# A two-layer trunk on one core: taps ahead of the heads, an end by tiles, meta values in fewer matmuls, meta rows on ACT, squares in other slots

## The chip, the cores and the metric

One core of one Trainium2 chip runs the whole program. The metric is the device time of one execution in microseconds. The engines are PE (matmuls; PEld is its weight load), DVE, ACT, POOL and SP, which here issues transfers; each works through its own list of instructions in the order in which the list was built, and waits for others by semaphores.

## The reference

512 tokens of 1024 features, with 16 learned meta tokens ahead of them (528 positions), go through an input norm and two layers. A layer is half a feed-forward net, a token mixer, and half a feed-forward net, each added to its scaled input and normed:

```
h = LN(alpha*h + 0.5*SwiGLU_1(h))
h = LN(alpha*h + W_out [pool | conv | retention](h))
h = LN(alpha*h + 0.5*SwiGLU_2(h))

z = h @ w_in                               # pool 256, conv 2 x 256, q, k, v, g 512 each
pool : trailing means over 2, 4, 8, 16 tokens minus the input, times w_pool
conv : u = a * sigmoid(gate); depthwise causal convolution, 31 taps; LN; silu; @ w_pw
ret  : 4 heads of 128; q, k turned by cos/sin; in chunks of 64 with decay;
       norm over the head; * gain * silu(g)
```

The meta tokens are dropped from the output. All is float32.

## The kernel before, in words

Activations lie with features on the partitions, and positions in two halves (s = 0 and 1) of 264 columns: 256 tokens and 8 meta columns. Every product of two float32 matrices is made of three matmuls: each operand is split into a high part, rounded to the matmul's format on ACT (L91, L315), and a low part, the difference, on DVE or POOL (L94, L320); then high x high, high x low and low x high are added in one PSUM bank (L133 to L135). PSUM has four banks under the tag "acc", two each under "att" and "stat". SBUF tiles come from pools by tag: 16 buffers of the tag "wide" (558 columns), 4 of "q", 5 of "sm", and so on. A tile that is asked for takes the buffer that comes free next, in the order in which the program asks.

The order on each engine is set when the program is built: a scheduler takes the instructions in the order of the code, with its own estimate of when each can start, and puts the ready ones into each engine's list. What the code yields and when (`PACE`) shifts them.

`enter` norms the input rows token by token; of two tiles of meta rows (8 rows each) it lets POOL do the scaling (L244), of the others DVE or ACT (L242, L246). PE turns them (L257). `center` norms features: sum over tiles, mean by a matmul (L283), centring on DVE (L289), squares on ACT into tiles of the tag "q" (L291), sums of the squares on POOL and DVE (L296, L298), variance by a matmul (L189).

The mixer makes first the pool and convolution inputs (m0pu, m0u), then the values v0 to v4, token tile by token tile: L680 to L682 multiply 128 tokens (v4: the 16 meta positions) with w_v, 8 x 3 matmuls of 512 columns. v4's tokens stand in small tiles xm, filled by POOL (L670). DVE sums each value tile over a head (L684), ACT centres it (L690). Then the heads run through `work`: per head two projections each for k and q (m0kp, m0qp: 24 matmuls of 264 columns), turned by `rotary` (ACT L701, L702, DVE L703 to L705), k's meta columns copied by POOL (L794, m0km), then scores (L719), decay on DVE (L730), values, gates (m0gp).

The convolution's 31 taps for two halves of 128 channels are 62 instructions on DVE (L608 the first two, L610 the others), each over 528 columns into m0y, a wide tile. `conv_taps` yields after each, and the loop over the heads takes `PACE[head]` of them per step of `work`: 4, 3, 3, 2 and 0. The pooling windows (L639, L642, on POOL; L645 to L647 on DVE) are sums of shifted copies. The layer 1 mixer (m1) does the same.

The last feed-forward net (`last_ffn`) turns h to token tiles first. Its five parts multiply hidden units with w2, both operands split; output columns are taken in two halves (`ch`), and in the last part the second half is done tile by tile (L888 to L890), DVE adding each product to yt (L894). Then `measure`, `root`, `scale` and `leave` norm each of the four token tiles and send it out (L938, L944, L948 to L956).

Of the kernel before, what the change touches and what calls it, by code (L numbers as in the profile page):

```python
# [58 lines left out]
def trunk(ctx, tc, a):  # L59
# [786 lines left out]
    def last_ffn(l, name):  # L846
# [18 lines left out]
        for part, units in enumerate(PARTS):  # L865
# [5 lines left out]
            nk = len(full)  # L871
            for ch in range(2):
# [24 lines left out]
                if part == len(PARTS) - 1 and ch == 1:  # L897

                    for tt in range(3):
                        for i in steps:  # L900
                            step(i, tt)
                        for j in range(2):
                            add(tt, j, ps[tt][:, j * 256 : (j + 1) * 256])
                    for j in range(2):
                        o = ps[3] if j == 0 else acc(f"{name}o{ch}4")
                        for i in steps:
                            step(i, 3, j * 256, 256, o[:, :256])
                        add(3, j, o[:, :256])
                else:
                    for i in steps:  # L910
                        for tt in range(4):
                            step(i, tt)
                    for tt in range(4):
                        for j in range(2):
                            add(tt, j, ps[tt][:, j * 256 : (j + 1) * 256])
# [158 lines left out]
```

## Time and profile before

| what | value |
|---|---|
| runs | 1963.27, 1964.85, 1964.92 us; median 1964.85 |
| the profiled execution | 1963.63 us; its span 1961.8 us |
| granted clock of PE, mean | 0.994 |
| PE busy | 1907.0 us, 97% of the span, 14471 matmuls |
| DVE busy | 1526.4 us, 78% |
| ACT busy | 909.2 us, 46% |
| POOL busy | 217.4 us, 11% |
| chain that ended last | PE 82%, DVE 11%, issue 2%, ACT 2%, POOL 2% |

The span is the profiled part of one execution; the time is some 1.8 us longer. The chain is the work that ended last, followed back step by step. Where an engine that is busy most of the span stands still, the row of the instruction behind the gap names what it waited for. An idle engine that nobody waits for costs nothing.

### The profile page before, as it was taken

What the parts mean: (1) busy time and instruction counts of PE and PEld (TensorE: products, weight loads), DVE (VectorE), ACT (ScalarE), POOL (GpSimd) and SP (SyncE); (2) the same over time, 40 slices, a digit from 0 to 9 for tenths busy, and PEclk for the clock granted to TensorE, in tenths of its full rate; (3) what the DMA queues carried; (4) which work ended last, traced back from release to release, by engine and by line L of the source; (5) the groups of instructions that cost most, each with busy time, mean ns of one, the idle gap of its engine ahead of it and who ended that gap; (6) DMA issues with size and microseconds to landing.
All of it is one profiled execution on the core that took longest, in us unless ns stands there. A gap on an engine that the chain in (4) does not pass through costs nothing.

```text
span 1961.8 us, 36780 instructions
## 1 busy us (share of the span) xinstructions
PE 1907.0 (97%) x14471; PEld 1824.0 (93%) x14471; DVE 1526.4 (78%) x3426; ACT 909.2 (46%) x1817; POOL 217.4 (11%) x283
## 2 busy tenths in 40 slices
PE   7999999999999999999999999999999999999996
PEld 6999999897899999999999999998889999999995
DVE  7788778689767887778696788787897686877787
ACT  5454446444333644455464454454343265544461
POOL 4000000442003000000120000005320130000001
PEclk9999999999999999999999999999999999999998
DMA  4422323322112223223223323332231213323321
GB/s 144 130 89 95 119 87 105 101 76 86 63 33 76 65 97 119 87 97 105 90 71 103 108 81 103 98 129 65 65 105 55 65 44 119 119 76 108 108 97 43
DMA packets 61068, 177.98 MB, mean 91 GB/s; under 512 B 6976, under 2 KB 10944, under 8 KB 60896
## 3 DMA queue, kind: packets, MB, share of 16 engines
q1 hardware_dynamic: 59744, 174.59, 27.9%
q8 instruction: 113, 1.85, 0.4%
q10 hardware_dynamic: 1152, 1.05, 0.2%
q14 instruction: 59, 0.48, 0.1%
HBM read 173.52 MB, written 2.10 MB: 90 GB/s over the span
## 4 chain that ended last, share of the span: by engine, by line
PE 82%; DVE 11%; issue 2%; ACT 2%; POOL 2%; DMA 0%; SPq 0%; DVEq 0%; POOLq 0%; ACTq 0%
PE f1bo L890 2%; PE f1bo L888 2%; PE f1bo L889 2%; PE f1a_y L134 2%; PE f0a_y L134 2%; PE f0b_y L134 2%; PE f1a_y L135 2%; PE f0b_y L133 2%; PE f0b_y L135 2%; PE f1a_y L133 2%; PE f0a_y L133 2%; PE f0a_y L135 2%; DVE m1y L610 1%; PE m1sc L719 1%; PE m0o L738 1%
## 5 line engine op out<-in xcount | busy, mean ns | idle before, releaser
L610 DVE SCALAR_TENSOR_TENSOR m1y<-m1u,vec,m1y 128x528 f32<-128x528 f32 x60 | 46.1, 803 | 0.0
L91 ACT CAST f0b_o_h<-f0b_o_r 128x512 fp32r<-128x512 f32 (+1 forms) x37 | 23.4, 636 | 48.7 <-PE f0b_y L134 29.6
L91 ACT CAST f0a_o_h<-f0a_o_r 128x512 fp32r<-128x512 f32 (+1 forms) x37 | 23.4, 635 | 48.6 <-PE f0a_y L134 29.5
L610 DVE SCALAR_TENSOR_TENSOR m0y<-m0u,vec,m0y 128x528 f32<-128x528 f32 x60 | 45.9, 801 | 0.0
L91 ACT CAST f1a_o_h<-f1a_o_r 128x512 fp32r<-128x512 f32 (+1 forms) x37 | 23.4, 636 | 48.4 <-PE f1a_y L134 29.6
L335 DVE TENSOR_TENSOR x<-x,f0a_y 128x264 f32<-128x264 f32 x64 | 27.2, 426 | 23.2 <-PE f0a_y L135 23.1
L335 DVE TENSOR_TENSOR h<-h,f1a_y 128x264 f32<-128x264 f32 x64 | 27.1, 425 | 23.1 <-PE f1a_y L135 23.0
L335 DVE TENSOR_TENSOR h<-h,f0b_y 128x264 f32<-128x264 f32 x64 | 27.1, 425 | 23.0 <-PE f0b_y L135 22.9
L94 DVE TENSOR_TENSOR f1bw_l<-f1bw_r,f1bw_h 128x512 fp32r<-128x512 f32 x42 | 27.7, 688 | 17.6 <-ACT f1bw_h L91 17.0
L949 POOL TENSOR_TENSOR yt<-yt,g_last 128x256 f32<-128x256 f32 x4 | 3.0, 739 | 333.2 <-ACT yt L948 333.2
L94 DVE TENSOR_TENSOR f0a_o_l<-f0a_o_r,f0a_o_h 128x512 fp32r<-128x512 f32 (+1 forms) x42 | 26.7, 642 | 13.8 <-ACT f0a_o_h L91 11.7
L94 DVE TENSOR_TENSOR f0b_o_l<-f0b_o_r,f0b_o_h 128x512 fp32r<-128x512 f32 (+1 forms) x42 | 26.6, 642 | 13.8 <-ACT f0b_o_h L91 11.7
L94 DVE TENSOR_TENSOR f1a_o_l<-f1a_o_r,f1a_o_h 128x512 fp32r<-128x512 f32 (+1 forms) x42 | 26.7, 642 | 13.7 <-ACT f1a_o_h L91 11.4
L278 POOL TENSOR_TENSOR f0b_ln_s<-h,h 128x264 f32<-128x264 f32 x2 | 1.6, 820 | 310.0 <-DVE h L335 310.0
L587 POOL MEMSET m0u<- 128x30 f32 x2 | 0.2, 123 | 304.0 <-PE f0a_20Q L135 304.0
L587 POOL MEMSET m1u<- 128x30 f32 x2 | 0.2, 123 | 303.1 <-PE f1a_20Q L135 303.1
L894 DVE TENSOR_TENSOR yt<-yt,f1bo 128x256 f32<-128x256 f32 x80 | 27.8, 415 | 5.4 <-PE f1bo L890 5.3
L91 ACT CAST f1bw_h<-f1bw_r 128x1024 fp32r<-128x1024 f32 (+1 forms) x22 | 22.1, 1011 | 21.1 <-PE f1bo L890 4.2
L291 ACT ACTIVATE m_ln_q<-h 128x264 f32<-128x264 f32 (+1 forms) x32 | 11.9, 414 | 39.7 <-DVE h L289 36.2
L257 PE MATMUL tr<-ident,xtok 128*128 128x128 f32 (+1 forms) x48 | 10.9, 328 | 11.9 <-DVE xtok L242 11.3
L257 PEld LDWEIGHTS tr<-ident,xtok 128*128 128x128 f32 (+1 forms) x48 | 6.8, 167 | 16.0 <-issue 14.7
L281 POOL TENSOR_TENSOR m_ln_s<-m_ln_s,h 128x264 f32<-128x264 f32 (+1 forms) x20 | 18.3, 914 | 30.8 <-DVE h L329 24.8
(10715 smaller groups left out, 9301.2 us busy)
## 6 DMA issues: line engine op xcount, KB each, us to landing
f1bw_r<-in_w2last SPq DMA_DIRECT2D x20, 512.0 KB, 3.9
f0a_o_r<-in_w SPq DMA_DIRECT2D x32, 256.0 KB, 2.7
f0b_o_r<-in_w SPq DMA_DIRECT2D x32, 256.0 KB, 2.8
f1a_o_r<-in_w SPq DMA_DIRECT2D x32, 256.0 KB, 2.8
m0wo_r<-in_w_out SPq DMA_DIRECT2D x8, 512.0 KB, 3.5
m1wo_r<-in_w_out SPq DMA_DIRECT2D x8, 512.0 KB, 3.5
m0w_r<-in_w_in SPq DMA_DIRECT2D x6, 512.0 KB, 4.0
m1w_r<-in_w_in SPq DMA_DIRECT2D x6, 512.0 KB, 4.2
```

The lines of the kernel that those rows point to most:

```text
L91: nc.scalar.copy(out=hi[:, :n], in_=w[:, :n])
L94: e.tensor_tensor(out=lo[:, sl], in0=w[:, sl], in1=raw(hi[:, sl]), op=ALU.subtract)
L133: nc.tensor.matmul(out, lhsT=wh, rhs=xh, start=start, stop=False, skip_group_check=onto)
L134: nc.tensor.matmul(out, lhsT=wh, rhs=xl, start=False, stop=False, skip_group_check=onto)
L135: nc.tensor.matmul(out, lhsT=wl, rhs=xh, start=False, stop=stop, skip_group_check=onto)
L335: nc.vector.tensor_tensor(out=y, in0=y, in1=ps, op=ALU.add)
L610: nc.vector.scalar_tensor_tensor(out=ys[c], in0=src, scalar=wk, in1=ys[c], op0=ALU.mult, op1=ALU.add)
L719: nc.tensor.matmul(sc[:kn, :cw], lhsT=kk[ks][:, kc : kc + kn], rhs=qq[s][:, c0 : c0 + cw], start=True, stop=True)
L888: nc.tensor.matmul(o, lhsT=hh, rhs=wh, start=part > 0 and i == 0, stop=False)
L889: nc.tensor.matmul(o, lhsT=hh, rhs=wl, start=False, stop=False)
L890: nc.tensor.matmul(o, lhsT=hl, rhs=wh, start=False, stop=i == nk - 1)
L894: nc.vector.tensor_tensor(out=y[:, :256], in0=y[:, :256], in1=o, op=ALU.add)
```

## The change

Five edits come together.

1. Taps: `EARLY` = 28 taps are made before the loop over the heads, and `PACE` becomes (1, 1, 2, 2, 0); inside the loop the taps are asked for behind the last rotary or gate (`issue_after`).
2. Meta values: xm holds high and low of the 16 meta positions side by side as 48 columns (16 high, 16 of zero, 16 low; the zeros are written by POOL, L666), so that v4 takes two matmuls per k instead of three; the low part's rows are then copied by ACT into a new wide tile m0vm and added by DVE.
3. Meta rows: in `enter` ACT scales them too, and the order within a group is turned round.
4. End by tiles: the last part's products run per token tile over both halves, followed at once by that tile's norm; tiles 0 to 2 leave by ACT, POOL (tile 2: DVE) and DVE, tile 3 by DVE, ACT and POOL.
5. Squares: every second square of a norm over more than two tiles takes a slot of the tag "sm", the one of the scores, instead of "q".

```diff
-PACE = (4, 3, 3, 2, 0)
+EARLY, PACE = 28, (1, 1, 2, 2, 0)
...
-            for i, tt in enumerate(group):
+            for i, tt in reversed(list(enumerate(group))):
...
-                elif i == 2:
-                    nc.gpsimd.tensor_scalar(out=y, in0=y, scalar1=mv[:p, i, 0:1], scalar2=rs[:p, i : i + 1], op0=ALU.subtract, op1=ALU.mult)
...
-            q.append(t(f"{name}_q{i}", "q"))
+            q.append(t(f"{name}_q{i}", "sm" if k > 2 and i % 2 else "q"))
...
-            pair = sq_pool.tile([P, 2, NM], F32R, tag="xm", name=f"{name}xm{k}", bufs=KT)
+            pair = sq_pool.tile([P, 48], F32R, tag="xm", name=f"{name}xm{k}", bufs=KT)
+            nc.gpsimd.memset(raw(pair[:, NM:32]), 0.0)
...
+                if tt == 4:
+
+                    nc.tensor.matmul(ps[:48], lhsT=xm[k], rhs=wh, start=k == 0, stop=False)
+                    nc.tensor.matmul(ps[:48], lhsT=xm[k], rhs=wl, start=False, stop=k == KT - 1)
+                    continue
...
+            if tt == 4:
+                vm = wide(f"{name}vm")
+                nc.scalar.copy(out=vm[:n, :512], in_=ps[32 : 32 + n])
+                nc.vector.tensor_tensor(out=vm[:n, :512], in0=ps[:n], in1=vm[:n, :512], op=ALU.add)
+                ps = vm[:, :512]
...
         taps = conv_taps()
+        for _ in range(EARLY):
+            next(taps)
...
-                for _ in range(PACE[hd]):
-                    next(taps, None)
                 if hd == HEADS or i > 0:
                     next(steps, None)
+                with tc.issue_after(made["last"]):
+                    for _ in range(PACE[hd]):
+                        next(taps, None)
...
+        c0 = done * 512
+        w_last = [[], []]
+        for i in range(0, nk, 2):
+            cw = min(2, nk - i) * 512
+            for ch, make in enumerate((weights, weights_wide)):
+                w = make(a["w2last"][ch, :, c0 + i * 512 : c0 + i * 512 + cw], cw, f"{name}l{ch}{i}")
...
         for tt in range(4):
+            ts = slice((tt % 2) * P, (tt % 2 + 1) * P)
+            for ch in range(2):
+                for c, cw in ((0, 256), (256, 256)) if (tt, ch) == (3, 1) else ((0, 512),):
+                    o = acc(f"{name}l{tt}{ch}{c}")
...
             measure(tt)
             root(tt)
-            if tt == 3:
-                with tc.issue_after(met[tt]):
-                    leave(2)
             scale(tt)
-            if tt != 2:
-                leave(tt)
+            leave(tt)
```

DVE's list in layer 0's mixer, before, from the centring value of v3's sum to the first rotary (L684 sums a value tile, L610 is a tap, L94 the low part of a weight tile, L703 the first product of a rotary; m0vmu is a value tile's mean, m0wq, m0wk and m0wg are weights):

```order
L685 TENSOR_SCALAR m0vmu_5671<-m0vmu_5671 128x4
L610 SCALAR_TENSOR_TENSOR m0y_5475<-m0u_5184,vec,m0y_5475 128x528
L94 TENSOR_TENSOR m0wq_l<-m0wq_r,m0wq_h 128x512 x2
L610 SCALAR_TENSOR_TENSOR m0y_5474<-m0u_5114,vec,m0y_5474 128x528
L94 TENSOR_TENSOR m0wk_l<-m0wk_r,m0wk_h 128x512 x2
L684 TENSOR_REDUCE m0vmu_5705<-m0v_5680 16x4
L94 TENSOR_TENSOR m0wg_l<-m0wg_r,m0wg_h 128x512
L685 TENSOR_SCALAR m0vmu_5705<-m0vmu_5705 16x4
L94 TENSOR_TENSOR m0wg_l<-m0wg_r,m0wg_h 128x512
L94 TENSOR_TENSOR m0wq_l<-m0wq_r,m0wq_h 128x512 x2
L610 SCALAR_TENSOR_TENSOR m0y_5475<-m0u_5184,vec,m0y_5475 128x528
L703 TENSOR_TENSOR m0k00r<-m0kp_0_5738,cosb 128x264
```

The same list after, from v3's sum on (L693 sums a value tile, L606 and L608 are taps, m0vm the meta rows' new tile):

```order
L693 TENSOR_REDUCE m0vmu_5679<-m0v_5654 128x4
L694 TENSOR_SCALAR m0vmu_5679<-m0vmu_5679 128x4
L94 TENSOR_TENSOR m0wq_l<-m0wq_r,m0wq_h 128x512 x2
L94 TENSOR_TENSOR m0wk_l<-m0wk_r,m0wk_h 128x512 x2
L606 TENSOR_SCALAR m0y_5474<-m0u_5114,vec 128x528
L690 TENSOR_TENSOR m0vm<-m0v_5688,m0vm 16x512
L606 TENSOR_SCALAR m0y_5475<-m0u_5184,vec 128x528
L693 TENSOR_REDUCE m0vmu_5708<-m0vm 16x4
L608 SCALAR_TENSOR_TENSOR m0y_5474<-m0u_5114,vec,m0y_5474 128x528
L694 TENSOR_SCALAR m0vmu_5708<-m0vmu_5708 16x4
```

And where that stretch of taps ends (L714 to L716 are a rotary, L643 to L645 the end of the pooling windows):

```order
L608 SCALAR_TENSOR_TENSOR m0y_5474<-m0u_5114,vec,m0y_5474 128x528
L608 SCALAR_TENSOR_TENSOR m0y_5475<-m0u_5184,vec,m0y_5475 128x528
L643 TENSOR_TENSOR m0sm_2_5754<-m0sm_2_5754,inv_n 128x16
L645 SCALAR_TENSOR_TENSOR m0xp_5247<-m0sm_2_5754,inv_n,m0xp_5247 128x512
L644 TENSOR_TENSOR m0xp_5247<-m0sm_2_5754,m0xp_5247 128x16
L714 TENSOR_TENSOR m0k00r<-m0kp_0_5769,cosb 128x264
L715 TENSOR_TENSOR m0k00r_5795<-m0k00r_5795,sinb 128x264
L714 TENSOR_TENSOR m0k01r<-m0kp_0_5803,cosb 128x264
L716 TENSOR_TENSOR m0k00r<-m0k00r,m0k00r_5795 128x264
```

Before, taps stand between the sums and the splits; after, they are one block between the second wk split and the first rotary.

POOL's list in layer 0's mixer, before (L670 fills the meta tiles xm, L642 and L639 are the pooling windows m0sm, m0xp their input):

```order
L670 CAST m0xm_5511<-f0a_ln_x7h 128x8
L670 CAST m0xm_5511<-f0a_ln_x7l 128x8
L642 TENSOR_TENSOR m0sm_1_5720<-m0xp_5247 128x542
L639 COPY m0sm_2_5723<-m0sm_1_5720 128x2
L642 TENSOR_TENSOR m0sm_2_5723<-m0sm_1_5720 64x541
L639 COPY m0sm_1_5891<-m0xp_5418 128x1
```

The same list after, from there on (L666 zeroes the middle columns of xm, here for layer 1; L637 and L640 are the windows):

```order
L666 MEMSET m1xm_17799 128x16
L666 MEMSET m1xm_17805 128x16
L666 MEMSET m1xm_17811 128x16
L637 COPY m0sm_1_5751<-m0xp_5247 128x1
L640 TENSOR_TENSOR m0sm_1_5751<-m0xp_5247 128x542
L637 COPY m0sm_2_5754<-m0sm_1_5751 128x2
L640 TENSOR_TENSOR m0sm_2_5754<-m0sm_1_5751 64x541
```

The eight fills for layer 1's tiles (the last three are shown), which take layer 0's buffers, now stand ahead of the windows.

DVE's list at the end, before, behind the last add of a product (L894; yt_20874 is tile 3's last quarter, L938 and L955 scale a tile, L169 to L172 are root steps):

```order
L894 TENSOR_TENSOR yt_20874<-yt_20874,f1bo_24134 128x256
L172 SCALAR_TENSOR_TENSOR f1brs_g<-f1brs_w,f1brs_g 128x1
L210 BN_AGGR f1bmv_24243<-f1b_st 128x2
L209 BN_STATS f1b_st<-yt_20874 128x6
L169 SCALAR_TENSOR_TENSOR f1brs_w<-f1brs_g,f1brs_y 128x1
L161 TENSOR_SCALAR f1brs_v<-f1bmv_24243 128x1
L938 SCALAR_TENSOR_TENSOR yt_20867<-yt_20867,f1bmv_24243,g_last_24151 128x256
L170 SCALAR_TENSOR_TENSOR f1brs_y<-f1brs_w,f1brs_y 128x1
L162 TENSOR_SCALAR f1brs_y<-f1brs_v,bits 128x1
L177 TENSOR_SCALAR f1brs_y<-f1brs_y 128x1
L938 SCALAR_TENSOR_TENSOR yt_20868<-yt_20868,f1bmv_24243,g_last_24153 128x256
L944 SCALAR_TENSOR_TENSOR f1bnb<-f1bmv_24202,f1brs_y 128x1
```

And after, around its last add (L983; yt_20873 to yt_20876 are tile 2, yt_20880 tile 3's last quarter, L953 and L954 the gain and the offset):

```order
L953 TENSOR_TENSOR yt_20873<-yt_20873,g_last_23957 128x256
L983 TENSOR_TENSOR yt_20880<-yt_20880,f1bl_24285 128x256
L954 TENSOR_TENSOR yt_20873<-yt_20873,b_last_23965 128x256
L953 TENSOR_TENSOR yt_20874<-yt_20874,g_last_23959 128x256
L953 TENSOR_TENSOR yt_20875<-yt_20875,g_last_23961 128x256
L954 TENSOR_TENSOR yt_20874<-yt_20874,b_last_23967 128x256
L954 TENSOR_TENSOR yt_20875<-yt_20875,b_last_23969 128x256
L953 TENSOR_TENSOR yt_20876<-yt_20876,g_last_23963 128x256
L209 BN_STATS f1b_st<-yt_20880 128x6
L954 TENSOR_TENSOR yt_20876<-yt_20876,b_last_23971 128x256
L210 BN_AGGR f1bmv_24302<-f1b_st 128x2
L161 TENSOR_SCALAR f1brs_v<-f1bmv_24302 128x1
```

After, only tiles 2 and 3 stand behind the last add; before, parts of tiles 1, 2 and 3 do.

## Rows read from the trace of the kernel before

**Rows 1.** the page's first lines, busy time of each engine (us, share, instructions):

```profile
span 1961.8 us, 36780 instructions
...
PE 1907.0 (97%) x14471; PEld 1824.0 (93%) x14471; DVE 1526.4 (78%) x3426; ACT 909.2 (46%) x1817; POOL 217.4 (11%) x283
```

**Rows 2.** PE's waits by line and releaser: total, times, longest:

```profile
PE m1sc L719 <- POOL m1km L794: 3.5, 1, 3.5
PE m0sc L719 <- POOL m0km L794: 3.4, 1, 3.4
PE f0a_ln_rs L189 <- DVE f0a_ln_q L298: 1.9, 1, 1.9
```

**Rows 3.** windows of 20 us around the first mixer, busy time by engine:

```profile
460.00:480.00 20.00, 16.29 (x111) 14.72 (x111) 20.00 (x41) 9.22 (x17) 12.29 (x4) 0.91 0.48 141
...
500.00:520.00 20.00, 19.99 (x130) 17.02 (x129) 15.52 (x44) 6.52 (x13) 2.13 (x4) 1.00 0.20 57
```

**Rows 4.** timeline of DVE, layer 0's mixer (start, length, what, idle before):

```profile
430.55 5.38 DVE L610 SCALAR_TENSOR_TENSOR m0y<-m0u,vec,m0y 128x528 f32<-128x528 f32 x5
...
448.20 4.15 DVE L610 SCALAR_TENSOR_TENSOR m0y<-m0u,vec,m0y 128x528 f32<-128x528 f32 x6
...
454.31 1.28 DVE L94 TENSOR_TENSOR m0wq_l<-m0wq_r,m0wq_h 128x512 fp32r<-128x512 f32 x2
...
461.15 0.41 DVE L703 TENSOR_TENSOR m0k00r<-m0kp,cosb 128x264 f32<-128x264 f32 x1
...
472.42 0.41 DVE L703 TENSOR_TENSOR m0k10r<-m0kp,cosb 128x264 f32<-128x264 f32 x1
```

**Rows 5.** timeline of PE, the same stretch:

```profile
446.29 0.40 PE L680 MATMUL m0v<-m0wv_h,m0xm 128*16 128x512 f32 x1
...
451.82 0.28 PE L133 MATMUL m0kp<-f0a_ln_x0h,m0wk_h 128*128 128x264 f32 x1
...
463.48 0.28 PE L133 MATMUL m0kp<-f0a_ln_x0h,m0wk_h 128*128 128x264 f32 x1
...
472.85 0.62 PE L719 MATMUL m0sc<-m0q00r,m0km 128*16 128x264 f32 x2 [3.38 <-POOL m0km L794]
...
474.54 0.42 PE L135 MATMUL m0gp<-f0a_ln_x0h,m0wg_l 128*128 128x264 f32 x1
...
477.20 0.28 PE L133 MATMUL m0gp<-f0a_ln_x3h,m0wg_h 128*128 128x264 f32 x1
```

**Rows 6.** timeline of ACT, the same stretch:

```profile
454.76 1.06 ACT L91 CAST m0wk_h<-m0wk_r 128x1024 fp32r<-128x1024 f32 x1
```

**Rows 7.** timeline of POOL, from the norm to the first copies:

```profile
401.45 0.19 POOL L670 CAST m0xm<-f0a_ln_x0h 128x8 fp32r<-128x8 f32 x1 [3.98 <-ACT f0a_ln_x0h L315]
...
419.64 1.26 POOL L642 TENSOR_TENSOR m0sm<-m0xp 128x542 f32<-128x542 f32 x1 [11.97 <-ACT m0xp L597]
...
432.26 1.74 POOL L642 TENSOR_TENSOR m0sm<-m0sm 64x535 f32<-64x535 f32 x1
463.06 3.76 POOL L794 COPY m0km<-m0k00r 128x8 f32<-128x8 f32 x1 [29.06 <-DVE m0k00r L705]
466.77 6.03 POOL L794 COPY m0km<-m0k01r 128x8 f32<-128x8 f32 x1
```

**Rows 8.** timeline of POOL, the start:

```profile
10.64 4.45 POOL L244 TENSOR_SCALAR xtok<-xtok,in_mv,in_y 8x512 f32<-8x512 f32 x2 [9.31 <-DVE in_y L177]
```

**Rows 9.** timeline of PE, the start:

```profile
19.09 0.59 PE L134 MATMUL f0a_0p<-x_l,f0a_0a_h 128*128 128x264 f32 x1
```

**Rows 10.** timeline of DVE, behind the last product:

```profile
1944.31 0.42 DVE L894 TENSOR_TENSOR yt<-yt,f1bo 128x256 f32<-128x256 f32 x1
...
1947.38 0.69 DVE L170 SCALAR_TENSOR_TENSOR f1brs_y<-f1brs_w,f1brs_y 128x1 f32<-128x1 f32 x1
...
1956.79 1.74 DVE L955 SCALAR_TENSOR_TENSOR yt<-yt,f1brs_y,b_last 128x256 f32<-128x256 f32 x3
```

**Rows 11.** timeline of ACT, second half of f0a's norm:

```profile
392.61 0.43 ACT L291 ACTIVATE f0a_ln_q<-x 128x264 f32<-128x264 f32 x1 [0.41 <-POOL f0a_ln_q L296]
```

More of the change, by code (lines that the diff above doesn't have):

```diff
@@ L704, in rotary @@
             nc.vector.tensor_tensor(out=r2[:, :n], in0=r2[:, :n], in1=sinb[:, s, :n], op=ALU.mult)
-            nc.vector.tensor_tensor(out=r[:, :n], in0=r[:, :n], in1=r2[:, :n], op=ALU.add)
+            made["last"] = nc.vector.tensor_tensor(out=r[:, :n], in0=r[:, :n], in1=r2[:, :n], op=ALU.add).ins
             return r
@@ L767, in gate @@
             g = t(f"{name}gs{hd}{s}", "g")
-            nc.scalar.activation(g[:, : no[s]], ps[:, : no[s]], AF.Silu)
+            made["last"] = nc.scalar.activation(g[:, : no[s]], ps[:, : no[s]], AF.Silu).ins
             gg.append(g)
@@ L871, in last_ffn @@
             nk = len(full)
+            if part == len(PARTS) - 1:
+                break
             for ch in range(2):
@@ L896, in last_ffn @@
                 steps = range(-1 if part == 0 else 0, nk)
[L897 to L903, printed above, removed]
-                    for j in range(2):
[L905 to L915, printed above, removed]
+                for i in steps:
+                    for tt in range(4):
+                        step(i, tt)
+                for tt in range(4):
+                    for j in range(2):
+                        add(tt, j, ps[tt][:, j * 256 : (j + 1) * 256])
             done += nk
@@ L935, in scale @@
             for j, y in enumerate(yt[tt]):
-                if tt == 1:
+                if tt < 3:
                     break
@@ L941, in leave @@
             g_, b_ = gb
-            if tt == 1:
-                nb = sq_pool.tile([P, 3], F32, tag="nb", name=f"{name}nb", bufs=2)[:, :1]
+            if tt < 3:
+                nb = sq_pool.tile([P, 3], F32, tag="nb", name=f"{name}nb{tt}", bufs=2)[:, :1]
                 nc.vector.scalar_tensor_tensor(out=nb, in0=mvs[tt][:, 0:1], scalar=-1.0, in1=rss[tt], op0=ALU.mult, op1=ALU.mult)
@@ L946, in leave @@
                 y = yt[tt][j][:, :256]
-                if tt == 1:
+                if tt < 3:
                     nc.scalar.activation(y, y, AF.Identity, scale=rss[tt], bias=nb)
-                    nc.gpsimd.tensor_tensor(out=y, in0=y, in1=g_[j][:, :256], op=ALU.mult)
-                    nc.gpsimd.tensor_tensor(out=y, in0=y, in1=b_[j][:, :256], op=ALU.add)
-                elif (tt, j) in ((2, 1), (2, 3), (3, 3)):
+                    e = nc.gpsimd if tt < 2 else nc.vector
+                    e.tensor_tensor(out=y, in0=y, in1=g_[j][:, :256], op=ALU.mult)
+                    nc.vector.tensor_tensor(out=y, in0=y, in1=b_[j][:, :256], op=ALU.add)
+                elif j % 2:
                     nc.scalar.mul(y, y, rss[tt])
@@ L956, in leave @@
                 (nc.sync if j % 2 else nc.scalar).dma_start(out=a["out"][tt * P : (tt + 1) * P, j * 256 : (j + 1) * 256], in_=y)
-        for tt in range(4):
+        c0 = done * 512
[4 more added lines that the diff above has]
+                w = make(a["w2last"][ch, :, c0 + i * 512 : c0 + i * 512 + cw], cw, f"{name}l{ch}{i}")
+                w_last[ch] += w if ch else [at(w, slice(c, c + 512)) for c in range(0, cw, 512)]
+        for tt in range(4):
+            ts = slice((tt % 2) * P, (tt % 2 + 1) * P)
+            for ch in range(2):
+                for c, cw in ((0, 256), (256, 256)) if (tt, ch) == (3, 1) else ((0, 512),):
+                    o = acc(f"{name}l{tt}{ch}{c}")
+                    for i in range(nk):
+                        wh, wl = (x[:, c : c + cw] for x in w_last[ch][i])
+                        hh, hl = at(hid[full[i]][tt // 2], ts)
+                        nc.tensor.matmul(o[:, :cw], lhsT=hh, rhs=wh, start=i == 0, stop=False)
+                        nc.tensor.matmul(o[:, :cw], lhsT=hh, rhs=wl, start=False, stop=False)
+                        nc.tensor.matmul(o[:, :cw], lhsT=hl, rhs=wh, start=False, stop=i == nk - 1)
+                    for k in range(0, cw, 256):
+                        y = yt[tt][2 * ch + (c + k) // 256]
+                        nc.vector.tensor_tensor(out=y[:, :256], in0=y[:, :256], in1=o[:, k : k + 256], op=ALU.add)
             measure(tt)
             root(tt)
-            if tt == 3:
-                with tc.issue_after(met[tt]):
-                    leave(2)
             scale(tt)
-            if tt != 2:
-                leave(tt)
+            leave(tt)
     load_tokens((4, 0, 1))
```

7 lines of the change are left out of this document (4 added, 3 removed).

## The prediction

> **What bounds the kernel now.** First the page's busy shares: PE works 1907.0 us of a span of 1961.8 (97%), so idle PE time is the only thing to win or lose, and there are 54.8 us of it [rows 1]. Then PE's waits: in both mixers the first score waits 3.4 and 3.5 us for a small copy on POOL (m0km, m1km), and in a norm 1.9 us for the squares [rows 2]. Third, the window around the mixer's start: from 460 to 480 DVE is busy all 20.00 us while PE loses 3.7 [rows 3]. DVE is the second limit exactly where the taps are moved. Last, the tail: the last add on DVE starts at 1944.31, and DVE works until 1958.53 [rows 10].
>
> **The change part by part (times of layer 0).**
>
> ***Taps with meta values.*** Of a mixer's 62 taps most fill DVE between the sums of the value tiles before: 6 of them stand in 4.15 us at 448.20, 0.68 each [rows 4]. In the order after, the 28 early taps stand behind v3's reduce, both halves of the wq split and of the second wk split, and ahead of the first rotary (k00, L714). The cause is the new tile m0vm: it comes from the same 16 "wide" buffers as the convolution's sums m0y, is asked for earlier in the program, and is written only when v4 is done, so the taps are placed behind it. PE's order is the same on both sides: v4, k00, k01, q00, q01, k10, k11, scores. The projections take turns on four "acc" banks, so k10 needs the bank that the rotary of k00 reads. That wait costs nothing before: k00's rotary starts at 461.15 [rows 4], and k10 begins at 463.48, right behind q01 [rows 5].
>
> The sum for after. v4 runs from 446.29 to 451.82, 24 matmuls, 5.53 us [rows 5]; 16 make 3.69, so it ends at 449.98, and the four projections (451.82 to 463.48, 11.66 us) end at 461.64. On DVE v3's reduce and the wq split (1.2 us [rows 4]) come first; the wk cast on ACT (1.06 us [rows 6]) comes behind v3's centring, so the wk split ends near 450.6. Then the meta rows' add and reduce (1.3, an estimate from the splits' 0.6 for 512 columns) and 28 x 0.68 = 19.0 us of taps: 470.9.
>
> In layer 0 POOL adds to it. Eight small fills (L666) that zero layer 1's meta tiles wait for v4's matmuls to have read layer 0's, and in POOL's order they stand ahead of the pooling windows. Before, these windows ran from 419.64 to 434.00 [rows 7]. After, their 11 us or so lie at 450 to 461.5, beside the taps. Beside the windows 5 taps took 5.38 us, 1.08 each, against 0.68 without [rows 4]: some 8 taps at +0.4 make 3.0, and the block ends at 473.9. Three pooling operations (0.9) come next, and k00's L714 ends at 475.1. PE is idle from 461.6 to 475.1, **13.5 us**.
>
> k10 and k11 take 463.48 to 469.47, 6.0 us; after its 3.38 us of waiting PE ran at the low level until 477.20 (matmuls of 0.42 instead of 0.28 us, 0.22 apart instead of 0.12) [rows 5], which costs 4.35 x (1 - 0.12/0.22) = 2.0. The same here: k11 ends at 483.1. The first score also needs both copies of meta columns on POOL. Before they took 3.76 and 6.03 us for 8 columns, where another copy of this shape took 0.19 [rows 7]. With k00 rotated at 476.4 they end between 476.8 (0.19 each) and 486.2 (3.76 and 6.03). The second one ended at 472.80 just as an L703 of 0.41 us did, which reads PSUM [rows 4]; in the new order the rows of that kind come where the second copy would end at 482.7 (k10's) to 485.0 (k11's). I take 483.8, nearer to the long ones. The first score was at 472.85: 10.95 later, less the 2.0 that before paid behind it: **+9.0**. Layer 1 has no such fills, its windows stay early, the 3.0 go: **+6.0**. Bounds: +4.7 (no POOL delay, copies early) and +12.7 (copies at 486.2, the slow stretch once more) for layer 0, +4.7 and +9.7 for layer 1. The eight matmuls saved per layer (8 x 0.23 = 1.84 us) are in these sums and buy nothing: PE only arrives earlier at its wait.
>
> The Trainium skill (SBUF — State Buffer, "Who interferes with whom") says that a DVE instruction with two SBUF inputs contends with a GpSimd instruction that reads SBUF, and that one with at most one does not, outside the two-port modes. The 6.03 us beside back-to-back taps against 0.19 agree. By that rule alone the second copy waits for k11's L714, near 485.0, and layer 0 stands at +10.2.
>
> ***The later taps.*** 34 are left for the heads, so some 8 more than before run behind the first rotary, 5.4 us of DVE. From 500 to 520 DVE is busy 15.52 of 20 us [rows 3], which hides most of it: **+1**, bounds 0 and 4.
>
> ***End by tiles.*** PE does the same products, so they end near 1944.3 on either side. Before, 14.2 us of DVE follow the last add, because the norms of several tiles are crowded there with POOL beside them: a one-column L170 takes 0.69 us [rows 10]. After, tiles 0 and 1 leave under the matmuls. Behind the last add DVE's order has eight operations of tile 2 (2.8 us), the last statistics, four scalings and the root of tile 3 (5) and two last products (0.8), then POOL adds what ACT scaled (1.5): some 10 us, estimates from rows of 0.3 to 0.6 each like the last three products, 1.74 [rows 10]. DVE's work on one tile is about 7.5 us against PE's 7.0 for its 30 matmuls of 0.23, so it lags 1 to 2. **-3**, bounds -6 and 0.
>
> ***Meta rows.*** Before, POOL takes 4.45 us for the two 8-row tiles [rows 8], and its part of x_l and the 0u split come behind. After, ACT does them among its own. PE's dense stretch started at 19.09 [rows 9]; the transposes would be through some 2 us sooner, but the cast of 0u now stands behind x_7 on ACT and its split ends just where PE wants it. **-1.5**, bounds -3 and +1.
>
> ***Squares.*** In a norm's second half the last three squares wait up to 0.41 us each for POOL to give a slot back [rows 11], 1.0 in all. With other slots they come sooner, but the sums on DVE stand in a fixed order among other work, so 0.6 of it arrives at PE, in five norms that make it wait [rows 2]: **-3**, bounds -7 (four waits like f0a's gone) and 0.
>
> Sum: 9.0 + 6.0 + 1 - 3 - 1.5 - 3 = +8.5 on the profiled run's 1963.63 (span 1961.8 and 1.83 around it): 1972. The median of the runs is 1.2 above that run; I leave it out.
>
> **Rivals.** (a) The stall is worse: copies late, the clock low once more: 12.7 + 9.7 + 2 - 5 = +19, 1983. For it: the copy of 6.03 us. Against: DVE must wait for k10 and k11 itself, and a DVE that waits lets POOL through. (b) The savings eat the stall: layers at 4.7 + 5.7, the small parts at -3.5, -2.5, -4 with +1: +1, about 1965. For it: PE does wait at the norms. Against: those sums are held by DVE's order, not by slots alone. (c) Faster, decided by the tail: if tile 2 too is out of the way at the last add, only one tile's statistics, root and products remain (3.7 us of the 14.2), and the end gives 10.5; with layers at 9.4 and -4.5 from start and squares it is -5.6, 1958. It needs a DVE that doesn't lag; eight operations of tile 2 behind the last add in its order speak against it, and from a lag of 2 us on it is gone. (d) The taps do not come late: DVE's idle time ahead of v4 is used. Then the waits of 3.4 and 3.5 and the slow stretches behind them go, v4's 1.84 counts: -7 per layer, about 1943. The order excludes it.
>
> **How the numbers follow.** A change of less than 0.2% (3.9 us) can't be told from none. Forecast (+5 to +14) 0.52, (a) 0.17, (b) 0.19, (c) and (d) 0.12. Slower is the forecast with (a), rounded down: 0.68; same is (b), 0.20; faster is (c) and (d), 0.12. The range leaves out 2 in 10 and takes in (b) and most of (a): 1960 to 1983. The forecast's own range is 1968 to 1978.
>
> **What would show it.** PE should wait 11 to 13 us for DVE's L714 ahead of k10 in layer 0 and some 3 less in layer 1, DVE being idle during v0 to v3 and full from v4 on; the waits for m0km and m1km may stay at 1 to 3 us. POOL's windows should start at v4's end in layer 0 and stay early in layer 1. Behind the last add some 10 us should remain. It is wrong if taps stand among the value tiles in the trace, if k10 starts right behind q01, or if the start, the norms and the end give back more than 15 us.

## The result and the profile after

The kernel after took 1991.35 us (median of 4 runs, 1988.83 to 1992.25) against 1964.61 before: 1.0135 times as long, with an interval of 1.0118 to 1.0153. Slower, as forecast, but by 26.7 us where 8.5 were forecast, and above the range. The profiled execution's span grew by 27.6 us. The table shows by how much PE is late with the same work, against the profile of before, in this profile and in those of the experiments below (us, each to about 0.1; read from PE's tiles: the last f0a_21p at the start, the last product of m0pu and m1pu with x3h as a mixer begins, the first f0b_0p and f1b_0p behind it, and the span). A step from one column to the next is what that stretch costs.

| kernel | start | mixer 0 begins | block f0b begins | mixer 1 begins | block f1b begins | span |
|---|---|---|---|---|---|---|
| before, at | 54.1 | 411.9 | 626.1 | 1381.7 | 1590.2 | 1961.8 |
| after | +5.4 | +5.7 | +24.4 | +22.1 | +30.2 | +27.6 |
| rows_only | +5.4 | +6.4 | +7.3 | +6.6 | +7.3 | +7.7 |
| early_taps | +5.9 | +5.5 | +10.5 | +8.2 | +12.2 | +9.4 |
| early_windows | +4.2 | +3.8 | +8.7 | +7.2 | +13.5 | +10.7 |
| early_windows_no_rows | -0.3 | -0.7 | +4.8 | +2.4 | +9.2 | +6.2 |
| windows_before_fills | +5.2 | +4.9 | +13.1 | +11.7 | +19.7 | +17.0 |
| taps_only | -0.1 | -0.1 | -2.9 | -2.1 | -3.5 | -3.4 |
| meta_only | -0.5 | -0.3 | +9.1 | +7.8 | +23.1 | +23.2 |
| join_without_meta_values | +5.4 | +4.8 | +1.9 | +0.9 | -2.1 | -4.7 |
| sums_in_q_slots | +4.5 | +4.0 | -0.7 | -2.9 | -6.3 | -8.9 |
| meta_only_q_slots | -0.6 | -0.3 | +1.3 | +1.9 | +1.4 | +1.4 |
| end_and_squares | +1.1 | +1.6 | +1.6 | +0.5 | 0.0 | -2.6 |
| join_q_slots_no_meta_rows | -0.3 | -0.7 | -5.4 | -7.6 | -10.9 | -13.7 |

So after loses 5.4 at the start, 18.7 in layer 0's mixer and 8.1 in layer 1's; the blocks and norms between them give 2.3 and the end gives 2.6 back.

The first lines of the page answer to [rows 1]: PE is busy 5.8 us longer, with 16 matmuls fewer, and idle 76.6 instead of 54.8.

```profile
span 1989.4 us, 36764 instructions
...
PE 1912.8 (96%) x14455; PEld 1829.8 (92%) x14455; DVE 1530.1 (77%) x3431; ACT 915.3 (46%) x1832; POOL 203.5 (10%) x294
```

PE's waits answer to [rows 2] (total, times, longest). The small copies on POOL are gone from the top; the first rotary of each layer stands there, then two waits that the prediction did not have.

```profile
PE m0kp L133 <- DVE m0k00r L714: 13.6, 1, 13.6
...
PE m1kp L133 <- DVE m1k00r L714: 11.0, 1, 11.0
PE m0gp L135 <- DVE m0wg_l L94: 2.6, 1, 2.6
...
PE f0a_0p L134 <- POOL x_l L266: 2.2, 1, 2.2
```

DVE's timeline in layer 0 (start, length, what, idle before), against [rows 4]: idle 4.7 us ahead of each reduce of v1 to v3, then everything behind v4 at once, with 25 taps back to back ahead of the first rotary. The rotaries of k01 and q00 wait 2.56 and 1.01 us for ACT's copies, and the first half of the wg split comes behind them, at 493.63.

```profile
452.30 0.69 DVE L693 TENSOR_REDUCE m0vmu<-m0v 128x4 f32<-128x512 f32 x1 [4.68 <-PE m0v L686]
...
458.48 0.67 DVE L690 TENSOR_TENSOR m0vm<-m0v,m0vm 16x512 f32<-16x512 f32 x1
...
460.14 0.75 DVE L608 SCALAR_TENSOR_TENSOR m0y<-m0u,vec,m0y 128x528 f32<-128x528 f32 x1
460.89 17.05 DVE L608 SCALAR_TENSOR_TENSOR m0y<-m0u,vec,m0y 128x528 f32<-128x528 f32 x25
...
480.68 0.42 DVE L714 TENSOR_TENSOR m0k00r<-m0kp,cosb 128x264 f32<-128x264 f32 x1
...
484.87 0.43 DVE L714 TENSOR_TENSOR m0k01r<-m0kp,cosb 128x264 f32<-128x264 f32 x1 [2.56 <-ACT m0k01r L713]
...
487.68 0.43 DVE L714 TENSOR_TENSOR m0q00r<-m0qp,cosb 128x264 f32<-128x264 f32 x1 [1.01 <-ACT m0q00r L713]
...
493.63 0.68 DVE L94 TENSOR_TENSOR m0wg_l<-m0wg_r,m0wg_h 128x512 fp32r<-128x512 f32 x1
```

POOL's timeline, against [rows 7]: the last fill, then the windows, one of them 20.21 us long, from 458.69 until just behind the taps' end at 477.94. The two copies for the scores, 3.76 and 6.03 us before, are short now.

```profile
456.05 0.11 POOL L666 MEMSET m1xm<- 128x16 f32 x1 [0.42 <-PE m0v L681]
...
456.73 1.55 POOL L640 TENSOR_TENSOR m0sm<-m0xp 128x542 f32<-128x542 f32 x1
...
458.69 20.21 POOL L640 TENSOR_TENSOR m0sm<-m0sm 64x541 f32<-64x541 f32 x1
...
485.77 0.60 POOL L805 COPY m0km<-m0k00r 128x8 f32<-128x8 f32 x1 [0.69 <-DVE m0k00r L716]
488.51 0.67 POOL L805 COPY m0km<-m0k01r 128x8 f32<-128x8 f32 x1 [2.14 <-DVE m0k01r L716]
```

ACT's timeline: its copy for the last window waits 21.13 us for POOL, and behind it stand k01's copies, two casts (one of them the cast at 485.81, the second of wg) and q00's copies. The cast of the wg tile whose split PE then lacks is the first one, at 455.87, and was long done.

```profile
455.87 1.07 ACT L91 CAST m0wg_h<-m0wg_r 128x1024 fp32r<-128x1024 f32 x1
...
483.43 0.64 ACT L639 COPY m0sm<-m0sm 64x535 f32<-64x535 f32 x1 [21.13 <-POOL m0sm L640]
484.07 0.38 ACT L712 COPY m0k01r<-m0kp 64x264 f32<-64x264 f32 x1
...
485.81 1.05 ACT L91 CAST m0wg_h<-m0wg_r 128x1024 fp32r<-128x1024 f32 x1
486.88 0.38 ACT L712 COPY m0q00r<-m0qp 64x264 f32<-64x264 f32 x1
```

PE's timeline, against [rows 5]: three waits where before had one.

```profile
481.15 0.59 PE L133 MATMUL m0kp<-f0a_ln_x0h,m0wk_h 128*128 128x264 f32 x1 [13.56 <-DVE m0k00r L714]
...
490.30 0.60 PE L730 MATMUL m0sc<-m0q00r,m0km 128*16 128x264 f32 x2 [0.97 <-DVE m0q00r L716]
...
494.37 0.59 PE L135 MATMUL m0gp<-f0a_ln_x0h,m0wg_l 128*128 128x264 f32 x1 [2.60 <-DVE m0wg_l L94]
```

The windows of the same stretch (busy time of PE, its loads, DVE, ACT and POOL, then the granted clock): PE's clock is at its low level (1.2 GHz, 0.50) in 475 to 485, at the end of the long wait and behind it, and a second time in 495 to 500 behind the short one.

```profile
475.00:480.00 5.00, 0.00 (x0) 0.00 (x0) 4.01 (x8) 0.00 (x0) 4.94 (x3) 0.50 0.00 0
480.00:485.00 5.00, 3.85 (x17) 3.85 (x18) 2.44 (x4) 1.53 (x4) 4.73 (x7) 0.50 0.00 0
485.00:490.00 5.00, 4.32 (x33) 4.11 (x31) 3.99 (x10) 3.36 (x6) 1.34 (x3) 0.92 0.00 0
490.00:495.00 5.00, 2.10 (x9) 1.43 (x10) 5.00 (x13) 1.50 (x4) 0.28 (x1) 0.76 0.00 0
495.00:500.00 5.00, 5.00 (x18) 4.01 (x18) 3.60 (x9) 0.00 (x0) 0.58 (x2) 0.50 0.02 3
500.00:505.00 5.00, 5.00 (x23) 3.54 (x23) 2.46 (x5) 2.46 (x4) 0.00 (x0) 0.72 0.37 105
```

The start, against [rows 8, 9]: POOL is rid of the small rows, but it waits for ACT's cast of 0u, begins that split at 19.92 (15.07 before), and in its new order the last low part of x stands behind the splits of 1u and 21w. PE waits 2.18 us for it at 30.93, and the window around that has a clock of 0.68 (1.00 before).

```profile
19.92 1.28 POOL L94 TENSOR_TENSOR f0a_0u_l<-f0a_0u_r,f0a_0u_h 128x512 fp32r<-128x512 f32 x1 [3.48 <-ACT f0a_0u_h L91]
...
27.40 2.78 POOL L94 TENSOR_TENSOR f0a_21w_l<-f0a_21w_r,f0a_21w_h 128x512 fp32r<-128x512 f32 x2
30.13 0.74 POOL L266 TENSOR_TENSOR x_l<-x,x_h 128x264 fp32r<-128x264 f32 x1
```

```profile
30.93 0.39 PE L134 MATMUL f0a_0p<-x_l,f0a_0a_h 128*128 128x264 f32 x1 [2.18 <-POOL x_l L266]
```

```profile
30.00:35.00 5.00, 4.08 (x21) 4.08 (x22) 3.66 (x14) 3.14 (x6) 0.87 (x2) 0.68 0.65 240
```

The end, on DVE, against [rows 10]: 11.9 us from the last add to the span's end (17.5 before).

```profile
1977.52 0.41 DVE L983 TENSOR_TENSOR yt<-yt,f1bl 128x256 f32<-128x256 f32 x1
...
1984.07 0.88 DVE L959 SCALAR_TENSOR_TENSOR yt<-yt,f1brs_y,b_last 128x256 f32<-128x256 f32 x2
```

### The profile page after: what moved, and what is told of

It reads as the page before. It is cut to its first block, busy times and chain, and to the rows that moved or that the text cites. A ratio compares the mean times of both kernels' runs of the same rounds, so it can differ in the third digit from the quotient of the medians.

```text
span 1989.4 us, 36764 instructions
## 1 busy us (share of the span) xinstructions
PE 1912.8 (96%) x14455; PEld 1829.8 (92%) x14455; DVE 1530.1 (77%) x3431; ACT 915.3 (46%) x1832; POOL 203.5 (10%) x294
## 3 DMA queue, kind: packets, MB, share of 16 engines
q1 hardware_dynamic: 59744, 174.59, 27.6%
## 4 chain that ended last, share of the span: by engine, by line
PE 66%; issue 16%; DVE 10%; ACT 2%; POOL 2%; DMA 0%; POOLq 0%; ACTq 0%; DVEq 0%
PE f1a_y L134 2%; PE f0a_y L134 2%; PE f0b_y L134 2%; PE f0b_y L133 2%; PE f1a_y L133 2%; PE f1a_y L135 2%; PE f0a_y L133 2%; PE f0b_y L135 2%; PE f0a_y L135 2%; POOL m0sm L640 1%; DVE m1y L608 1%; PE m0o L749 1%; PE m0sc L730 1%; PE m1o L749 1%; PE m1sc L730 1%
## 5 line engine op out<-in xcount | busy, mean ns | idle before, releaser
L333 DVE TENSOR_TENSOR h<-h,f0b_y 128x264 f32<-128x264 f32 x64 | 27.1, 425 | 23.3 <-PE f0b_y L135 23.2
L333 DVE TENSOR_TENSOR x<-x,f0a_y 128x264 f32<-128x264 f32 x64 | 27.1, 425 | 23.2 <-PE f0a_y L135 23.0
L333 DVE TENSOR_TENSOR h<-h,f1a_y 128x264 f32<-128x264 f32 x64 | 27.1, 425 | 23.1 <-PE f1a_y L135 23.0
L608 DVE SCALAR_TENSOR_TENSOR m0y<-m0u,vec,m0y 128x528 f32<-128x528 f32 x60 | 43.1, 755 | 0.0
L608 DVE SCALAR_TENSOR_TENSOR m1y<-m1u,vec,m1y 128x528 f32<-128x528 f32 x60 | 43.0, 756 | 0.0
L953 POOL TENSOR_TENSOR yt<-yt,g_last 128x256 f32<-128x256 f32 x8 | 6.1, 785 | 320.7 <-ACT yt L951 320.1
L94 DVE TENSOR_TENSOR f0a_o_l<-f0a_o_r,f0a_o_h 128x512 fp32r<-128x512 f32 (+1 forms) x42 | 26.7, 643 | 13.8 <-ACT f0a_o_h L91 11.7
L94 DVE TENSOR_TENSOR f1a_o_l<-f1a_o_r,f1a_o_h 128x512 fp32r<-128x512 f32 (+1 forms) x42 | 26.7, 643 | 13.8 <-ACT f1a_o_h L91 11.7
L94 DVE TENSOR_TENSOR f0b_o_l<-f0b_o_r,f0b_o_h 128x512 fp32r<-128x512 f32 (+1 forms) x42 | 26.7, 642 | 13.5 <-ACT f0b_o_h L91 11.4
L94 DVE TENSOR_TENSOR f1bw_l<-f1bw_r,f1bw_h 128x512 fp32r<-128x512 f32 x32 | 20.9, 689 | 9.5 <-ACT f1bw_h L91 9.1
L640 POOL TENSOR_TENSOR m0sm<-m0sm 64x541 f32<-64x541 f32 (+3 forms) x4 | 23.7, 5933 | 0.2
L91 ACT CAST f1bw_h<-f1bw_r 128x1024 fp32r<-128x1024 f32 x16 | 16.7, 1051 | 12.3 <-PE f1b_6Q L134 1.8
L910 DVE TENSOR_TENSOR yt<-yt,f1bo 128x256 f32<-128x256 f32 x64 | 21.9, 415 | 0.0
```

Of the source, the lines that this page charges most:

```text
L91: nc.scalar.copy(out=hi[:, :n], in_=w[:, :n])
L94: e.tensor_tensor(out=lo[:, sl], in0=w[:, sl], in1=raw(hi[:, sl]), op=ALU.subtract)
L333: nc.vector.tensor_tensor(out=y, in0=y, in1=ps, op=ALU.add)
L608: nc.vector.scalar_tensor_tensor(out=ys[c], in0=src, scalar=wk, in1=ys[c], op0=ALU.mult, op1=ALU.add)
L640: nc.gpsimd.tensor_tensor(out=dst[b:, w_:], in0=cur[b:, w_:], in1=cur[b:, : W - w_], op=ALU.add)
L910: nc.vector.tensor_tensor(out=y[:, :256], in0=y[:, :256], in1=o, op=ALU.add)
```

## The experiments

Three theories, and the kernels that tell them from their rivals. **A**: the meta values' new wide tile (m0vm) puts the taps behind v4, and the loss in the mixers comes from that. **D**: the meta rows' edit itself costs the 5.4 us at the start, through POOL's order. **F**: layer 0 loses 10.6 more than layer 1 through the fills, which hold POOL's windows until v4. The rivals stand in the quotes; letters that the first four quotes use otherwise are explained in them. Ratios are against the kernel before on the same chip.

**early_taps.** After, with the early taps requested ahead of the values:

```diff
+        taps = conv_taps()
+        for _ in range(EARLY):
+            next(taps)
         xm = []
```

> The changed kernel with one thing moved: the 28 early taps are asked for ahead of the values, so that the convolution's sums get their wide buffers before the meta rows' tile does. Theory A (that tile holds the taps back, and they then hold k00's rotary): the waits of 13.6 and 11.0 us ahead of k10 go, about 1960 us or below; the start stays 5.4 later; POOL's windows in layer 0 still come behind the fills. Rival B (28 taps are too many there, wherever they come from): the waits stay, 1985 or more.

1972.86 us, 1.0042 [1.0028, 1.0056]. The waits of 13.6 and 11.0 are gone, and so are 18.5 us. But the time is not the quote's 1960, nor rival B's 1985: the mixers still lose 5.0 and 4.0 us. PE now waits elsewhere for DVE, in layer 0 for a product between the scores, in layer 1 for wv's split, most of which stands behind the 28 taps:

```profile
PE m0sc L734 <- DVE m0sm L745: 5.1, 1, 5.1
PE m1v L689 <- DVE m1wv_l L94: 5.0, 1, 5.0
```

**early_windows.** As early_taps, and both layers' pooling windows requested ahead of the values too:

```diff
+        pool_y = {c: pool_windows(c) for c in range(2)}
         xm = []
```

> As the one before, and the pooling windows are asked for ahead of the values too. Theory A with fills: now the windows run under the value tiles in both layers and ACT's copy for them holds nobody; 1 to 4 us faster than the one before, about 1953. Rival B: 1985 or more. Rival C (the fills and the windows behind them cost nothing of their own, all of layer 0's extra 10 us came from the taps): the same time as the one before.

1974.36 us, 1.0051 [1.0037, 1.0064]: no better than early_taps, where the quote had 1953. Now both layers wait 7.8 us for wv's split. Requesting earlier moves the jam on DVE, it does not dissolve it; as it moved, this run can't tell what the fills cost (the quote's rival C).

```profile
PE m1v L690 <- DVE m1wv_l L94: 7.8, 1, 7.8
PE m0v L690 <- DVE m0wv_l L94: 7.8, 1, 7.8
```

**early_windows_no_rows.** The same with the meta rows' edit undone (GpSimd normalizes the 8-row tiles again, in the old order).

> As the one before, with the meta rows scaled as before the change. Theory D (the start's 5.4 us come from the order that ACT's meta rows bring: the last low part of x behind three weight splits on POOL): 5 to 6 us faster than the one before, about 1948, and first products of f0a end as in the kernel before. Rival E (the start's loss comes from the fills of xm or from something else of the join): no difference.

1969.84 us, 1.0031 [1.0019, 1.0042]: 4.5 us less, all of it at the start (-0.3 instead of +4.2). The quote's 1948 stood on the forecast for the run before and missed with it.

**rows_only.** Before with the meta rows' edit alone.

> The kernel before with the meta rows' edit alone. Theory D: slower by 5 to 6 us, about 1970, with PE waiting some 2 us for a low part of x from POOL and running at the low level behind it. Rival E: no slower than before, 1961 to 1965.

1969.13 us, 1.0025 [1.0015, 1.0036]: 4.2 us by the medians. The start is late by 5.4, with the same wait as in after; the further 2.3 of its profile lie where no edit does. That the edit costs this is shown. That it does so through POOL's order is read from the trace: ACT's order changed in the same edit (the 0u cast starts at 18.80 in after, at 12.12 before), and no run parts the two.

```profile
31.02 0.39 PE L134 MATMUL f0a_0p<-x_l,f0a_0a_h 128*128 128x264 f32 x1 [2.18 <-POOL x_l L266]
```

**windows_before_fills.** After with one thing moved on POOL:

```diff
-            nc.gpsimd.memset(raw(pair[:, NM:32]), 0.0)
+            with tc.issue_after(entered["pw"]) if "pw" in entered else nullcontext():
+                nc.gpsimd.memset(raw(pair[:, NM:32]), 0.0)
```

(entered["pw"] is the last addition of the windows.)

> The changed kernel with one thing moved: the eight fills of layer 1's meta tiles are issued behind layer 0's pooling windows on POOL instead of ahead of them; PE, DVE and ACT keep their orders. Theory F (in layer 0 the fills hold POOL's windows until v4, a window operation then runs beside 25 back-to-back taps and takes 20 us, ACT's copy of that window stands ahead of the wk and wg casts, and the late wg split and a second slow stretch follow): layer 0 becomes like layer 1, its loss goes from 18.7 to 8 to 10 us, the time from 1991.4 to about 1982 (1979 to 1985); the L133 wait goes from 13.6 to about 11, the wait for m0wg_l goes, no POOL operation of 64x541 takes over 5 us. Rival G (layer 0 loses more for another reason, the taps themselves or the clock that it enters with): within 3 us of 1991, the wait for m0wg_l stays.

1979.83 us, 1.0081 [1.0068, 1.0093]. Layer 0 loses 8.2 instead of 18.7, layer 1 8.0 (8.1 in after). The wait for m0wg_l is gone, the 64x541 operation takes 1.09 us, and the taps' block is as long as in after (25 in 17.05):

```profile
PE m1kp L133 <- DVE m1k00r L715: 10.9, 1, 10.9
PE m0kp L133 <- DVE m0k00r L715: 10.8, 1, 10.8
```

```profile
426.45 1.09 POOL L640 TENSOR_TENSOR m0sm<-m0sm 64x541 f32<-64x541 f32 x1
```

F stands: the fills ahead of the windows cost 10.5 us. Of these, 3.9 come up to the first score (2.8 in the first wait) and 6.6 behind it. One link of the quote is wrong: the wg split is not late through its cast, which ended at 456.9 in after, 37 us ahead of it. DVE itself is late: from k00's L714 to the split it takes 12.95 us in after and 8.34 here, and 3.6 of the difference are the waits for ACT's copies of k01 and q00. The links behind the window (ACT's copy, those waits, the second low clock) were moved together and not tried one by one.

**taps_only.** Before with EARLY, PACE and the taps' place behind made["last"].

> The kernel before with the taps' edits alone (28 early taps, the slower pace, the order behind the last rotary); the meta values as before. Theory A (the stall needs taps and meta values together, since only the new wide tile puts the taps behind the value tiles): 28 taps lie ahead of and among the value tiles, no wait of over 5 us for L705 ahead of k10, fewer taps in the heads: 1960 (1955 to 1966). Rival B (28 early taps jam DVE by themselves, here ahead of the second half of the wv split): a wait of 5 us or more for a wv low part or a first rotary in each layer, 1970 or more.

1959.85 us, 0.9979 [0.9970, 0.9988]: faster, as A has it. The taps lie among the value tiles, and the waits for the copies on POOL (3.5 and 3.4) are gone.

**meta_only.** Before with the meta values alone.

> The kernel before with the meta values' edits alone (48 columns, 16 matmuls instead of 24 in v4, the wide tile vm); taps paced as before. Theory A (the wide tile moves all 62 taps behind v4, but without the 28 asked for at once they stand in ones to threes between the rotaries): no wait of 10 us, but each rotary comes some 2 us later, so PE waits 2 to 6 us in all ahead of k10 to the first scores, and 30 to 40 taps run in the heads instead of 26: 1970 (1966 to 1978). Rival C (the wide tile alone makes the stall, whatever the taps' pace): a wait of 10 us or more for the first rotary, 1978 or more. Rival H (the shorter v4 counts and the taps hide): 1960 to 1963.

1985.47 us, 1.0106 [1.0092, 1.0120]. My 1970 missed: the time is that of rival C, at another place. All 62 taps lie behind v4, in ones to threes between the rotaries; k10 does not wait, but a later score (128x128, the third of its head) waits 10.0 us for a product on DVE behind them.

```profile
PE m0sc L730 <- DVE m0sm L741: 12.6, 3, 10.0
PE m1sc L730 <- DVE m1sm L741: 12.3, 3, 8.4
```

So the jam doesn't need the 28 early taps; they only decide which instruction waits in it.

**join_without_meta_values.** After with the meta values undone.

> The changed kernel with the meta values' edits undone (taps, end by tiles, meta rows and squares stay). Theory A (taps with meta values make all of the loss in the mixers): mixers at or below before's, start +5.4, norms -2.3, end -2.5: about 1963 with mixers at before's, 1959 if the early taps save 2 per layer (1957 to 1966), no wait of over 5 us for a rotary. Rival B (early taps jam DVE by themselves): 1972 or more.

1958.49 us, 0.9971 [0.9960, 0.9983]. The mixers are 2.9 and 3.0 us faster than before's, though the start still loses 5.4.

**sums_in_q_slots.** After, with the meta sum in other buffers (the reduce by halves too):

```diff
-                vm = wide(f"{name}vm")
-                nc.scalar.copy(out=vm[:n, :512], in_=ps[32 : 32 + n])
-                nc.vector.tensor_tensor(out=vm[:n, :512], in0=ps[:n], in1=vm[:n, :512], op=ALU.add)
+                vm = [t(f"{name}vm{i}", "q") for i in range(2)]
+                for i, y in enumerate(vm):
+                    nc.scalar.copy(out=y[:n, :256], in_=ps[32 : 32 + n, i * 256 : (i + 1) * 256])
+                    nc.vector.tensor_tensor(out=y[:n, :256], in0=ps[:n, i * 256 : (i + 1) * 256], in1=y[:n, :256], op=ALU.add)
```

> The changed kernel with one thing replaced: the meta rows' sum m0vm lies in two q slots of 256 columns instead of one of the 16 wide buffers (so there are two copies, two adds and two reduces of half the size). Theory A (the loss in the mixers comes from the wide buffer alone, which the taps' sums take turns on; with another one DVE's order has the taps among the value tiles again and the windows stay early): waits of 13.6 and 11.0 gone, v4's saved matmuls buy up to 1.8 us per layer on top of the join without meta values (1958.5): 1956 (1952 to 1961). Rival K (the meta values cost by themselves: 48 columns, the add and the reduce ahead of the first rotary): 1965 or more with a wait for L719 of over 4 us.

1954.88 us, 0.9959 [0.9947, 0.9972]: 36.5 us less than after. This is A shown by the one edit that it names. DVE's timeline has the taps among the reduces again:

```profile
440.45 2.79 DVE L608 SCALAR_TENSOR_TENSOR m0y<-m0u,vec,m0y 128x528 f32<-128x528 f32 x4
...
444.59 0.68 DVE L698 TENSOR_REDUCE m0vmu<-m0v 128x4 f32<-128x512 f32 x1
...
458.23 0.41 DVE L719 TENSOR_TENSOR m0k00r<-m0kp,cosb 128x264 f32<-128x264 f32 x1
```

**meta_only_q_slots.** Before with the meta values alone, their sum in q slots.

> The kernel before with the meta values alone, their sum in two q slots. Theory A: none of the 12.6 and 12.3 us that the first scores waited in the run of the meta values alone; v4 1.8 us shorter in each layer, of which the waits at the first scores (3.4 and 3.5 us before) leave something: 1962 (1957 to 1966). Rival K: 1972 or more.

1964.47 us, 1.0002 [0.9993, 1.0011]. The 12.6 and 12.3 are gone, but scores wait 4.4 and 4.5 us for m0sm and m1sm on DVE: with before's pace of taps, v4's saved matmuls buy nothing. With the early taps they may buy something (mixers at -4.7 and -3.4 in sums_in_q_slots, -2.9 and -3.0 without meta values), but these are single profiles, and the intervals of the two runs overlap.

**end_and_squares.** Before with these two parts.

> The kernel before with the end by tiles and the squares' slots alone. If the milestones read from the changed kernel (norms -2.3, end -2.5) are these two edits' own: 1964 - 4.8 = 1959 (1957 to 1961). If the earlier delays of the changed kernel made room for them (a later PE finds its squares ready): 1962 or more.

1959.41 us, 0.9976 [0.9967, 0.9985]: 4.8 us by the medians, as the milestones of after said. In its profile the end gives 2.6 and the stretch from block f0b to mixer 1 1.1 (2.3 in after, 1.4 in windows_before_fills); the +1.1 at its start, where no edit lies, shows what one profile can be off.

**join_q_slots_no_meta_rows.** All but the meta rows, the sum in q slots.

> All parts but the meta rows, the meta sum in two q slots. Theories A and D (the meta rows' edit costs 4.5 to 5.4 at the start) together: 1956 - 4.6 = 1951.5 (1947 to 1956), faster than the kernel before by some 0.6%. If the meta rows' cost is taken back by waits later: 1955 or more.

1949.86 us, 0.9932 [0.9919, 0.9944]: faster than both kernels, by 14.4 us than before.

## Why the prediction was wrong

The direction and the cause were right: the wide tile holds the taps, as said, and PE waited 13.56 us for k00's L714 in layer 0 (13.5 forecast) and 11.0 in layer 1. Two terms were not. The span's 27.6 less the forecast 8.5 is 19.1, of which the two layers with the later taps make 10.7 (26.7 against 16), the meta rows 6.9, the squares 1.0 (with the 0.3 ahead of mixer 0) and the end 0.4, but for rounding.

**"+9.0" for layer 0** failed: 18.7, above the bound of 12.7. (The bounds were not what their terms give either: copies at 486.2 with the slow stretch once more make 13.4, and no delay by POOL 5.3 where I had 4.7.) The first score came 11.7 us later (17.4 less the 5.7 on entry) where I had 10.95; what I lacked is behind it, where I had 2.0 given back and 6.9 more were lost. I counted POOL's late windows only as a drag on the taps, "some 8 taps at +0.4 make 3.0". The trace shows the reverse: the taps kept 0.68 each, and a window was held 20.21 us. I had followed the windows to DVE's pooling operations, not to ACT, where a copy of the last window stands ahead of k01's copies, two casts and q00's copies. DVE waits 3.6 us for these copies, its list comes later by that, and with it wg's split: PE waits 2.60 for the low part, and the second slow stretch follows (0.50 in 495 to 500, 0.72 behind it; 1.00 in windows_before_fills), the "clock low once more" that I had put into the bound and rival (a). windows_before_fills takes 10.5 away; I had sized the fills at 3.0. That the first wait came out right was luck in part: the block began at 460.14 (454.4 without the entry's 5.7; I had 451.9 from 450.6 and 1.3), but two of the 28 taps were done by then; it was not stretched by 3.0, and its pooling operations came late.

**"-1.5" for the meta rows** failed with its sign: +5.4, outside -3 to +1. I had looked at what PE waits for first. What counted was the low part of x that comes last. Before, POOL did it at 22.35, ahead of the splits of 1u and 21w:

```profile
22.35 0.75 POOL L268 TENSOR_TENSOR x_l<-x,x_h 128x264 fp32r<-128x264 f32 x1 [0.54 <-ACT x_h L266]
23.29 2.98 POOL L94 TENSOR_TENSOR f0a_1u_l<-f0a_1u_r,f0a_1u_h 128x512 fp32r<-128x512 f32 x2 [0.20 <-ACT f0a_1u_h L91]
```

After, POOL takes the splits first, and it starts at 30.13. The splits themselves begin late: ACT scales the meta rows and casts 0u only at 18.80 (12.12 before). I had seen that cast, but followed it only to the 0u split, not through POOL to what stands behind. PE's wait is 2.2 of the 5.4, and the clock of 0.68 takes some 1.6 in its window of 5 us (an estimate); the rest lies ahead of the wait and was not taken apart.

**Layer 1, +6.0**, measured 8.1 with the later taps in it (7 with their +1, bound 9.7). **Squares, -3**: -2.0 in after; PE's waits for L189 at the three norms of the blocks fell from 1.9 [rows 2], 1.8 and 1.8 to 1.0 each, but those at the norms behind the mixers rose from 1.6 to 2.6 in all, in the profile of every run with this edit, which I had not foreseen. **End, -3**: -2.6. The 17.5 us behind the last add became 11.9, but that add is 3.0 later than the rest of the block (33.2 against 30.2): DVE lags by 3.4 (0.04 before) behind PE's last product, recorded at 1973.82 and 0.28 long, where I assumed 1 to 2. **The copies on POOL** took 0.60 and 0.67 and no longer set the first score, which waited for the rotaries; my choice for them (483.8) decided nothing. It also stood on half a reading: both long copies of before ended with an L703, but each had run past an earlier one (at 464.82 and 470.19), and the second had only four taps beside it, among splits and rotaries.

Of the rivals, (a) had the right mechanism for the second loss, but at 1983 it was too small. (d) became true in sums_in_q_slots: with the taps ahead of v4 the waits go, worth 8.1 us in the mixers of the 14 given there. The range failed because two independent terms had bounds that ended at the effects I had traced; each was left by more than 4 us.

## What to carry to other kernels

A new buffer drawn from a shared rotating pool can move an unrelated chain of work behind its own writer; look up who else draws from the pool, and take another. When an engine's order changes, follow every reader of its late results on every engine in order, not only the one that the critical path is on. Work that is freed from a queue lets other entries go first: price the last item that the consumer needs, not the first.
